# Twelve instead of eight K tiles of an mLSTM input projection in seven products, with a tanh output gate and rescheduled DRAM sums

## The chip, the cores and the metric

The kernel runs on one core of a Trainium2 chip. The metric is device time in microseconds (us) of one execution of the whole program. Before the change it is 2150.58 us, the median of three runs (2148.87 to 2151.29). TensorE multiplies matrices into PSUM; VectorE (DVE), ScalarE (ACT) and GpSimd (POOL) work on tiles in SBUF and read PSUM where they can; SyncE (SP) issues most weight loads. Each engine runs its own instructions in order.

## The reference

An encoder trunk of two layers on 256 positions of width 2048, in float32. Layer 0 mixes by pooling and attention, layer 1 by an mLSTM; each is followed by a gated MLP of width 5632 with a short convolution. The change is in the mLSTM mixer, cut here to what matters:

```python
proj = h @ w_in                                   # 2048 -> 4*2048 + 32
q = heads(proj[..., :2048]) * 256 ** -0.5         # 8 heads of 256
k = heads(proj[..., 2048:4096])
v = heads(proj[..., 4096:6144])
o_gate = jax.nn.sigmoid(proj[..., 6144:8192])
...                                               # scans forward and backward
hsum = (h_fw + h_bw).transpose(0, 2, 1, 3)
hn = hsum * lax.rsqrt(jnp.mean(hsum * hsum, axis=-1, keepdims=True) + NORM_EPS)
hn = hn * h_norm.reshape(8, 256)
y = (hn.reshape(b, s, 2048) * o_gate)
return y @ w_out
```

## The kernel before, in words

**Numbers in two parts.** Each weight tile of 128 partitions and 1024 columns (512 KB) is loaded into a raw buffer (seven of them, `wraw`). `Stream.split` then cuts it into a high part (a cast by ScalarE, L137) and a low part (a subtraction by VectorE, L138) in one of four `hl` buffers. A product is three matmuls: high by high, high by low, low by high. `Stream` loads six tiles ahead of the one in use and splits two ahead.

**The order of TensorE** is written out by hand. `Weave` keeps a clock that the groups of matmuls advance by their nominal time, and runs queued generators (heads, gates, drains) when they are due. A number that a generator yields is the time until it goes on. The order of the other engines is worked out by the scheduler of the framework from the program and the dependencies.

**The mLSTM layer** (`mlstm_layer`, L780) works on four pairs of heads, `hp` 0 to 3. For each it runs, head by head, the projections of q (`mq`) and k (`mk`), 16 K tiles each, and then the output gate of this pair together with the values of the next (`gates_values`, L986); the last pair has only its gate (`mo`). A `head` generator (L868) per head makes the masked weights (`arg`), the scores (`qk`), the normalised matrix `A`, its transposes (`atr`) and the result (`av`, `hn`). `gated` (L929) applies the output gate. It makes the sigmoid from an Exp on ScalarE (L932), an addition of one (L936) and two reciprocals per head (L938) on VectorE, multiplies (L942) and transposes (`htr`).

**Seven products.** In `gates_values`, two K tiles, two halves of the positions and two column blocks (512 of the gate, 512 of the values) would take eight products. For the first eight K tiles (four pairs of K tiles, `ML_PAIRS`), a scheme of Strassen's kind takes seven. The list `ML_ORDER` (L48) gives their order. A stands for four products of one pair of K tiles on two weight tiles, B for two products on one tile, P for two products of two pairs on one tile. D and E are direct: four products each on one tile, for the K tiles that are not in the scheme. The scheme needs sums of blocks of x (`combine`, L956, kept in `mcomb`) and of weights. `first` and `second` put the partial results together on VectorE.

**Sums of weights.** An A needs the tiles s0 + s1 and s0 + s1 + r. They are made in DRAM ahead of time by `premix` (L478): copies issued by ScalarE's queue, accumulating DMAs issued by GpSimd's queue, each paced by a matmul. Where both tiles are made there (`Made`, `Made`) this takes ten DMAs per pair of K tiles. Where only the first is (`Made`, `Chain`), it takes four, and the second comes from two additions on VectorE in SBUF (L133 and L134). Before, even pairs are of the first kind and odd ones of the second. Calls of `premix` set the start and the gap between the pairs:

```python
premix(0, 26.0, 33.0, 8)              # sums of feed-forward layer 0, from the attention on
premix(2, 30.0, 30.0, 0)              # mLSTM sums, after up group 27 of 44 of that layer
hp == 0 and premix(1, 30.0, 30.0, 0)  # sums of feed-forward layer 1
```

**The feed-forward layers** interleave `up` groups (64 matmuls) with products of the same seven-product scheme (`pp`) and drains into PSUM and SBUF. The other products are `op` (output projections) and `dn` (direct down projections).

Of the kernel before, what the change touches and what calls it, by code (L numbers as in the profile page):

```python
# [9 lines left out]
F32 = mybir.dt.float32  # L10
F32R = mybir.dt.float32r
AF = mybir.ActivationFunctionType
# [4 lines left out]
P = 128  # L17
# [29 lines left out]
ML_PAIRS = 4  # L47
ML_ORDER = [(e[0], int(e[1:] or 0)) for e in "A0 D A1 D A2 D A3 D B0 B1 B2 E B3 E P0 E P2 E".split()]  # L48
# [171 lines left out]
def trunk(ctx: ExitStack, tc: tile.TileContext, gx, xT, xn, call, catt, cml, weights, mixes, out):  # L220
# [56 lines left out]
    def rsqrt(ss, n, scale, name):  # L277
# [502 lines left out]
    def mlstm_layer(norm, nxt):  # L780
        with ExitStack() as es:
# [6 lines left out]
            comb = actp.tile([P, ML_PAIRS, 2, 4, P], F32R, tag="B1", name="mcomb")  # L788
# [79 lines left out]
            def head(h, q, kk, vt, hh):  # L868
# [34 lines left out]
                yield 10.0 if h % 2 else 6.0  # L903
# [20 lines left out]
                r = rsqrt(ss, 2, 1.0 / MD, f"h{h}")  # L924
# [4 lines left out]
            def gated(ps, heads, og=None):  # L929
                og = og or t1p.tile([P, 2, len(heads) * MD], F32, tag="og", name=f"og{heads[0]}")  # L930
                for t in range(2):
                    a.activation(og[:, t, :], ps[:, t, :], AF.Exp, scale=nrcol[:, t : t + 1])  # L932
                yield 1.2
                for i, h in enumerate(heads):
                    o = og[:, :, i * MD : i * MD + MD]
                    v.tensor_scalar_add(o, o, 1.0)  # L936
                    for t in range(2):
                        tc.keep_in_program_order(v.reciprocal(o[:, t], o[:, t]))  # L938
# [3 lines left out]
                    tc.keep_in_program_order(v.tensor_mul(hn, hn, o))  # L942
# [13 lines left out]
            def combine(j):  # L956
# [9 lines left out]
                a.copy(comb[:, j, 0], sf)  # L966
                v.tensor_sub(comb[:, j, 1], sf, comb[:, j, 0].bitcast(F32))
# [18 lines left out]
            def gates_values(hp):  # L986
# [44 lines left out]
                for kind, j in ML_ORDER:  # L1031
                    if kind == "A":
                        xs = [[comb[:, j][:, i, m] for i in range(2)] for m in (1, 0, 2)] + [x_part(2 * j + 1, 1)]
                    elif kind == "B":
                        xs = [x_part(2 * j + k, 0) for k in range(2)]
                    elif kind == "P":
                        xs = [[comb[:, j + k][:, i, 3] for i in range(2)] for k in range(2)]
# [23 lines left out]
            for hp in range(MH // 2):  # L1061
# [12 lines left out]
                if hp == 0:  # L1074
                    nrcol = kp.tile([P, 2], F32, tag="nrcol", name="nrcol")
                    v.tensor_scalar_mul(nrcol, norm.rcol, -1.0)
# [9 lines left out]
                hp == 0 and premix(1, 30.0, 30.0, 0)  # L1086
# [7 lines left out]
    def ffn_layer(layer, norm, nxt):  # L1094
        with ExitStack() as es:
# [194 lines left out]
            for kind, c, i, *j in _ffn_plan(layer):  # L1290
                if kind == "up":
# [4 lines left out]
                    if layer == 0 and (c, i) == (len(FCH) - 3, 6):  # L1296
                        premix(2, 30.0, 30.0, 0)
# [72 lines left out]
def _ml_weights(chunks, parts):  # L1370
# [6 lines left out]
    for hp in range(MH // 2):  # L1377
# [4 lines left out]
        for kind, j in ML_ORDER:  # L1382
# [6 lines left out]
            out += made + [Chain(part[2])] * (j % 2)  # L1389
# [226 lines left out]
```

## Time and profile before

| | |
|---|---|
| median of three runs | 2150.58 us |
| profiled execution | 2149.47 us, of which the span of instructions 2147.7 us |
| TensorE busy | 2141.0 us, 100% of the span |
| VectorE busy | 1809.6 us, 84% |
| ScalarE busy | 1443.1 us, 67% |
| GpSimd busy | 289.4 us, 13% |
| DMA | 606.66 MB, mean 282 GB/s |
| mLSTM projections of q to k and the gates, pairs 0 to 2 | about 1000 to 1274 us |

The stages of interest, by the start of their matmuls: feed-forward layer 0 from 261 us, the mLSTM from 968 us, its three windows of gates and values from 1041, 1134 and 1228 us, its output projection from 1345 us, feed-forward layer 1 from 1444 us. A row of the chain of waits gives a start, a length and the work that the end of the program hung on at that time. A row of groups gives the line, the engine, the operation with its operands and count, then the busy time, the mean length in ns, and the idle time of the engine before it. Matmuls overlap, so TensorE's busy time alone doesn't show its rate; the distance between starts does.

### The profile page before, as it was taken

How to read it: one execution, taken by the hardware profiler on the slowest of the kernel's cores; microseconds unless marked ns; L12 is line 12 of the kernel's file. 1: busy time of each engine (PE TensorE's matmuls, PEld its weight loads, DVE VectorE, ACT ScalarE, POOL GpSimd, SP SyncE). 2: the span in 40 equal slices, each digit the busy share in tenths (PEclk: the TensorE clock that was granted, in tenths of full speed). 3: DMA queues.
4: the chain of work that ended last, by engine and by line, in shares of the span. 5: the costliest groups of instructions: out<-in, count | busy, mean ns of one | idle time of the engine just before them, and what ended most of it. 6: DMA issues, size and time to landing. Idle time of an engine off the chain costs nothing.

```text
span 2147.7 us, 32376 instructions
## 1 busy us (share of the span) xinstructions
PE 2141.0 (100%) x11364; PEld 1834.4 (85%) x11364; DVE 1809.6 (84%) x2548; ACT 1443.1 (67%) x2199; POOL 289.4 (13%) x366
## 2 busy tenths in 40 slices
PE   9999999999999999999999999999999999999999
PEld 8888888888888888889888888888888888888887
DVE  7786678889998889898888897667888898889988
ACT  6665577777777767766556564557777777777774
POOL 0022112111111121111100011211111111100000
DMA  9678889899999999888878798988999999988775
GB/s 333 209 213 257 260 250 320 272 326 328 320 330 328 331 341 320 296 292 213 287 232 282 234 308 238 280 244 245 311 293 331 333 314 319 287 256 270 253 251 188
DMA packets 181542, 606.66 MB, mean 282 GB/s; under 512 B 23706, under 2 KB 26562, under 8 KB 181378
## 3 DMA queue, kind: packets, MB, share of 16 engines
q1 hardware_dynamic: 133952, 478.60, 61.6%
q0 software_dynamic: 28384, 70.54, 19.2%
q10 hardware_dynamic: 19042, 55.45, 7.8%
q8 instruction: 89, 1.46, 0.3%
q14 instruction: 75, 0.61, 0.1%
HBM read 602.35 MB, written 104.90 MB: 329 GB/s over the span
## 4 chain that ended last, share of the span: by engine, by line
PE 95%; DVE 3%; DMA 1%; issue 1%; ACT 1%; ACTq 0%; DVEq 0%
PE up L275 44%; PE pp L275 15%; PE op L275 8%; PE mq L275 4%; PE mk L275 4%; PE mo L275 3%; PE qproj L275 3%; PE mv L275 3%; PE dn L275 3%; PE mp L275 1%; DVE hl L138 1%; PE kproj L275 1%; PE vproj L275 1%; PE pool L275 1%; PE qk L275 1%
## 5 line engine op out<-in xcount | busy, mean ns | idle before, releaser
L138 DVE TENSOR_TENSOR hl<-w,hl 128x1024 fp32r<-128x1024 f32 (+1 forms) x869 | 1046.1, 1215 | 161.2 <-ACT hl L137 154.1
L137 ACT CAST hl<-w 128x1024 fp32r<-128x1024 f32 (+1 forms) x868 | 891.7, 1046 | 395.4 <-PE up L275 112.6
L275 PE MATMUL up<-xx,hl 128*128 128x512 f32 (+1 forms) x5632 | 993.8, 337 | 0.0
L275 PEld LDWEIGHTS up<-xx,hl 128*128 128x128 f32 x5632 | 866.9, 188 | 130.4 <-DVE hl L138 0.5
L491 POOL DMA_DIRECT2D m<-m x184 | 148.6, 826 | 924.2 <-PE up L275 442.6
L275 PE MATMUL pp<-hl,s 128*128 128x512 f32 x912 | 227.8, 391 | 1.6 <-DVE hl L138 1.2
L275 PEld LDWEIGHTS pp<-hl,s 128*128 128x128 f32 x912 | 167.7, 188 | 37.3 <-DVE hl L138 4.9
L275 PE MATMUL pp<-hl,g 128*128 128x512 f32 x684 | 174.0, 390 | 0.0
L275 PEld LDWEIGHTS pp<-hl,g 128*128 128x128 f32 x684 | 125.8, 188 | 24.5
L441 ACT COPY tb_up<-up 128x512 f32<-128x512 f32 x88 | 51.6, 587 | 116.0 <-PE up L275 116.0
L1126 DVE TENSOR_TENSOR y<-y,z 128x510 f32<-128x510 f32 x88 | 60.7, 690 | 63.0 <-ACT y L1125 62.5
L491 POOL DMA_DIRECT2D m<-in_dn x80 | 70.0, 875 | 267.8 <-PE up L275 57.0
L1125 ACT ACTIVATE y<-tb_up,conv 128x256 f32<-128x256 f32 x176 | 103.8, 590 | 0.0
L275 PE MATMUL mk<-xx,hl 128*128 128x512 f32 (+1 forms) x512 | 92.5, 338 | 0.0
L442 DVE TENSOR_TENSOR tb_up<-up,tb_up 128x512 f32<-128x512 f32 x88 | 60.8, 690 | 37.4 <-ACT tb_up L441 37.1
L275 PE MATMUL mq<-xx,hl 128*128 128x512 f32 (+1 forms) x512 | 92.0, 337 | 0.0
L1123 ACT ACTIVATE z<-tb_up,conv 128x256 f32<-128x256 f32 x176 | 88.4, 502 | 5.3 <-DVE tb_up L1118 3.4
L275 PE MATMUL op<-hl,cat 128*128 128x512 f32 x384 | 91.5, 393 | 0.0
L275 PE MATMUL op<-hl,mcat 128*128 128x512 f32 x384 | 89.7, 392 | 0.0
L275 PEld LDWEIGHTS mq<-xx,hl 128*128 128x128 f32 x512 | 79.2, 188 | 11.6
L275 PEld LDWEIGHTS mk<-xx,hl 128*128 128x128 f32 x512 | 79.1, 188 | 11.4
L1124 ACT ACTIVATE z<-tb_up,conv 128x256 f32<-128x256 f32 x176 | 87.5, 497 | 0.0
(258 smaller groups left out, 2209.3 us busy)
## 6 DMA issues: line engine op xcount, KB each, us to landing
w<-in_up SPq DMA_DIRECT2D x352, 512.0 KB, 6.6
w<-in_dn SPq DMA_DIRECT2D x174, 512.0 KB, 6.0
w<-in_m_in SPq DMA_DIRECT2D x118, 512.0 KB, 5.3
w<-m SPq DMA_DIRECT2D x98, 512.0 KB, 5.7
m<-in_dn ACTq DMA_DIRECT2D x160, 256.0 KB, 5.7
m<-m POOLq DMA_DIRECT2D x184, 128.0 KB, 6.0
w<-in_a_in SPq DMA_DIRECT2D x45, 512.0 KB, 5.6
m<-in_dn POOLq DMA_DIRECT2D x80, 256.0 KB, 7.1
```

What stands on the lines that cost most here:

```text
L137: (self.nc.vector.tensor_copy if i + c == 0 else self.nc.scalar.copy)(hl[:, 0, c : c + n], w[:, c : c + n])
L138: low = self.nc.vector.tensor_sub(hl[:, 1, c : c + n], w[:, c : c + n], hl[:, 0, c : c + n].bitcast(F32))
L275: last_mm[0] = pe.matmul(out_, lhsT, rhs, start=start, stop=stop, skip_group_check=True)
L441: a.copy(tb, ps[:, :, 1, :])
L442: v.tensor_add(tb, ps[:, :, 0, :], tb)
L491: paced(eng.dma_start(to[p : p + P // 2], src[p : p + P // 2], **kw))
L1123: a.activation(z[:, 0, j, :], u[:, j, :], AF.Copy, scale=cw(tl, 0))
L1124: a.activation(z[:, 1, j, :], u[:, j, :], AF.Copy, scale=cw(tl, 2))
L1125: a.activation(y[:, j, :], u[:, j, :], AF.Identity, scale=cw(tl, 1), bias=cw(tl, 3))
L1126: v.tensor_add(y[:, :, 1:S], y[:, :, 1:S], z[:, 0, :, 0 : S - 1])
```

## The change

- `ML_PAIRS` goes from 4 to 6: K tiles 0 to 11 of the gate and the values of pairs 0 to 2 are in seven products, and only tiles 12 to 15 are direct. `ML_ORDER` is written anew. The sums of x for the two added pairs get a second buffer, `mcomb1`; the split q of a head gets one buffer in place of two.
- The sums for pair `hp` 2 are all of the kind `Made`, `Chain`.
- The sigmoid is written as half of one plus the tanh of half the argument. ScalarE takes Tanh; the addition of one is part of the multiplication on VectorE; the factor one half is put into the constants of `rsqrt`. The addition and the reciprocals go.
- The two generators' gaps between the matrix `A` and its transposes go from 6 and 10 to 9 and 14.
- The mLSTM sums start after up group 36 of feed-forward layer 0 instead of 27, and follow each other by 18 instead of 30. The sums of feed-forward layer 1 start after the gates of pair 1 instead of pair 0, by 28 instead of 30.

```diff
-ML_PAIRS = 4
-ML_ORDER = [(e[0], int(e[1:] or 0)) for e in "A0 D A1 D A2 D A3 D B0 B1 B2 E B3 E P0 E P2 E".split()]
+ML_PAIRS = 6
+ML_ORDER = [(e[0], int(e[1:] or 0)) for e in "A0 A1 D A2 A3 A4 D A5 B0 B1 B2 B3 B4 E B5 P0 P2 E P4".split()]
...
-        v.tensor_scalar(t, ss, scale, EPS, ALU.mult, ALU.add)
+        v.tensor_scalar(t, ss, scale / by**2, EPS / by**2, ALU.mult, ALU.add)
...
-            comb = actp.tile([P, ML_PAIRS, 2, 4, P], F32R, tag="B1", name="mcomb")
+            combs = [actp.tile([P, 4, 2, 4, P], F32R, tag="B1", name="mcomb0")]
+            combs.append(kp.tile([P, ML_PAIRS - 4, 2, 4, P], F32R, tag="mcomb", name="mcomb1"))
...
-                r = tp.tile([P, 2, 2, S], F32R, tag=name[0] + "hl", name=f"hl_{name}")
+                r = tp.tile([P, 2, 2, S], F32R, tag=name[0] + "hl", bufs=2 - (name[0] == "q"), name=f"hl_{name}")
...
-                yield 10.0 if h % 2 else 6.0
+                yield 14.0 if h % 2 else 9.0
...
-                r = rsqrt(ss, 2, 1.0 / MD, f"h{h}")
+                r = rsqrt(ss, 2, 1.0 / MD, f"h{h}", 0.5)
...
-                    a.activation(og[:, t, :], ps[:, t, :], AF.Exp, scale=nrcol[:, t : t + 1])
+                    a.activation(og[:, t, :], ps[:, t, :], AF.Tanh, scale=hrcol[:, t : t + 1])
...
-                    v.tensor_scalar_add(o, o, 1.0)
-                    for t in range(2):
-                        tc.keep_in_program_order(v.reciprocal(o[:, t], o[:, t]))
-                        yield 2.5
...
-                    tc.keep_in_program_order(v.tensor_mul(hn, hn, o))
+                    tc.keep_in_program_order(v.scalar_tensor_tensor(hn, o, 1.0, hn, ALU.add, ALU.mult))
...
-                hp == 0 and premix(1, 30.0, 30.0, 0)
+                hp == 1 and premix(1, 28.0, 28.0, 0)
...
-                    if layer == 0 and (c, i) == (len(FCH) - 3, 6):
-                        premix(2, 30.0, 30.0, 0)
+                    if layer == 0 and (c, i) == (len(FCH) - 2, 7):
+                        premix(2, 18.0, 18.0, 0)
...
-            made = [Made()] if j % 2 else [Made(), Made()]
+            made = [Made()] if j % 2 or hp == 2 else [Made(), Made()]
```

More of the change, by code (lines that the diff above doesn't have):

```diff
@@ L1032, in gates_values @@
                     if kind == "A":
-                        xs = [[comb[:, j][:, i, m] for i in range(2)] for m in (1, 0, 2)] + [x_part(2 * j + 1, 1)]
+                        xs = [[comb(j)[:, i, m] for i in range(2)] for m in (1, 0, 2)] + [x_part(2 * j + 1, 1)]
                     elif kind == "B":
@@ L1036, in gates_values @@
                     elif kind == "P":
-                        xs = [[comb[:, j + k][:, i, 3] for i in range(2)] for k in range(2)]
+                        xs = [[comb(j + k)[:, i, 3] for i in range(2)] for k in range(2)]
                     else:
@@ L1385, in _ml_weights @@
                 continue
-            made = [Made()] if j % 2 else [Made(), Made()]
+            made = [Made()] if j % 2 or hp == 2 else [Made(), Made()]
             part = [p[hp * ML_PAIRS + j] for p in parts]
             mixes.append(part + [made])
-            out += made + [Chain(part[2])] * (j % 2)
+            out += made + [Chain(part[2])] * (2 - len(made))
     return out, mixes
```

12 lines of the change are left out of this document (7 added, 5 removed).

## The prediction

> **What bounds the kernel now.** First the chain of waits. In it eighteen matmuls of 128x512 take 4.09 us, 0.227 us each, with no gap between pieces: TensorE's own issue rate is the time.
>
> ```profile
> 341.03 4.09 PE pp L275 x18
> ...
> 713.71 11.15 PE up L275 x64
> 734.90 3.84 DMA w<-in_up
> 745.28 10.05 DMA w<-in_dn
> 764.90 11.25 PE up L275 x64
> 776.15 4.09 PE pp L275 x18
> 780.24 11.14 PE up L275 x64
> ```
>
> The chain leaves TensorE in one place of weight, in the first feed-forward layer. Between 713.71 and 764.90 stand three groups of 64 (11.14 each) and 66 matmuls of products (18, 24 and 24): 33.4 + 15.0 = 48.4 us of work in 51.2 us. So 2.8 us are lost there, behind weights that landed 10 us after their issue.
>
> Then the stages, one row for each: length, busy time of TensorE, its weight loads, VectorE (DVE), ScalarE (ACT) and GpSimd (POOL), granted clock, DMA share, GB/s.
>
> ```profile
> 560.00:680.00 120.00, 120.00 (x643) 103.10 (x643) 108.02 (x143) 86.15 (x129) 19.17 (x24) 1.00 1.00 327
> 680.00:765.00 85.00, 83.70 (x439) 70.05 (x437) 72.63 (x96) 60.12 (x93) 16.88 (x21) 1.00 1.03 331
> 809.00:850.00 41.00, 41.00 (x219) 35.17 (x218) 38.27 (x52) 31.07 (x49) 8.06 (x10) 1.00 1.03 339
> 850.00:925.00 75.00, 75.00 (x400) 64.38 (x400) 65.50 (x83) 53.07 (x78) 7.02 (x9) 1.00 0.91 291
> 1000.00:1040.70 40.70, 40.70 (x242) 35.73 (x241) 32.65 (x63) 21.88 (x26) 3.87 (x5) 1.00 0.92 268
> 1040.70:1086.70 46.00, 46.00 (x224) 38.78 (x223) 41.60 (x69) 30.21 (x43) 6.25 (x8) 1.00 0.88 279
> 1133.60:1179.75 46.15, 46.15 (x221) 38.74 (x220) 41.23 (x67) 29.54 (x39) 3.54 (x5) 1.00 0.91 303
> 1227.70:1273.78 46.08, 45.40 (x215) 37.76 (x214) 41.00 (x66) 29.37 (x38) 6.52 (x8) 1.00 0.92 303
> 1273.78:1321.20 47.42, 47.42 (x286) 41.92 (x285) 39.22 (x61) 25.67 (x35) 7.90 (x10) 1.00 0.86 255
> ```
>
> Rows six to eight are the three gates-and-values windows that the change rewrites. TensorE is busy throughout except 0.68 us in the third. VectorE stands at 41.0 to 41.6 us, some 90%: it has 4.4, 4.9 and 5.1 us to spare per window, and that margin is what the change spends. The 0.68 us idle begins with a weight tile issued at 1225.21; what it costs stays in my sum, since the same queues meet there again.
>
> ```profile
> 1225.21 4.34 DMA w<-in_m_in
> ...
> 1231.31 3.70 PE mo L275 x15
> ```
>
> **Matmuls.** Per pair of heads the products go from 7x4 + 8x4 = 60 to 7x6 + 4x4 = 58. Three pairs save six products of three matmuls each, eighteen of 128x512: exactly the first row above, -4.09 us, all on the path.
>
> **Weight tiles and VectorE.** A window's tiles go from 8 (A) + 4 + 4 + 4 (B, D, E) + 2 (P) = 22 to 12 + 6 + 2 + 2 + 3 = 25. Each extra one costs a cast on ScalarE and a subtraction on VectorE. The tiles summed in SBUF ("Chain", two additions each) go from 2 per window to 3, 3 and 6.
>
> ```profile
> L138 DVE TENSOR_TENSOR hl<-w,hl 128x1024 fp32r<-128x1024 f32 x857 | 1036.5, 1221 | 160.9 <-ACT hl L137 153.8 <-DMA w<-in_m_out 3.0 <-DMA m<-in_dn 1.5
> ...
> L137 ACT CAST hl<-w 128x1024 fp32r<-128x1024 f32 x857 | 883.8, 1050 | 393.6 <-PE up L275 112.6 <-PE op L275 61.0 <-issue 29.8
> ...
> L133 DVE TENSOR_TENSOR w<-w,w 128x512 f32<-128x512 f32 x6 | 4.1, 683 | 0.0
> ```
>
> VectorE gets 3 x 1.22 = 3.7 us per window, and 2 x 0.68 = 1.37 us per further Chain: 1.4, 1.4 and 5.5 us. ScalarE gets 3 x 1.05 us on 30 of 46, beside other work.
>
> **The gate by tanh.** An addition and two reciprocals per head go; the multiply with the output gate becomes one with an addition inside, on the same operands, taken at the price of the third row.
>
> ```profile
> L938 DVE RECIPROCAL og<-og x16: 1692/1742/1746, 1085.1 to 1363.7; 128x256 f32<-128x256 f32 x16
> L936 DVE TENSOR_SCALAR og<-og x8: 418/419/427, 1083.3 to 1348.0; 128x512 f32<-128x512 f32 x8
> L942 DVE TENSOR_TENSOR hn<-hn,og x8: 675/682/685, 1094.5 to 1366.4; 128x512 f32<-128x512 f32 x8
> ```
>
> That is 0.42 + 2 x 1.74 = 3.9 us per head, 31 us of VectorE, but nearly all at the end of a window or after it, under the next heads' projections. Inside a window fall two of the additions and about one reciprocal: 2.6 us. The activation keeps its count and shape. If Tanh needed tables of its own, each group of gates between two Exp would load them twice, at most 8 loads; the nearest row is the load that Exp needed after Ln, 1283 ns.
>
> ```profile
> L833 ACT ACT_TABLE_LOAD x1 | 1.3, 1283 | 4.2 <-DMA gd<-gr 4.2
> ```
>
> I take no load. At both ends the path pays nothing: one load is shorter than the least cover of a weight tile, 2.1 us, shown next. The Trainium skill ("ScalarE: Activation LUTs", section on table sets) lists tanh beside exp in one set, so by it no load is added; no run here shows Tanh, and the reload after Ln shows that a function which the page places in a set with exp can still cost one.
>
> **The sum for VectorE.** First window: 41.6 + 3.7 + 1.4 - 2.4 (one addition and the larger part of a reciprocal less, by its end) = 44.2 of 46.0 - 1.36 = 44.6 us. Second: 41.2 + 3.7 + 1.4 - 2.6 = 43.7 of 44.8. Third: 41.0 + 3.7 + 5.5 - 2.6 = 47.6 of 44.7. The first two fit, just; the third is 2.8 us over. What is ready ahead helps little once tiles are used up every 1.36 us (six matmuls) instead of in turn with a D tile that lasts twelve:
>
> ```profile
> 1137.52 2.52 DVE L138 TENSOR_TENSOR hl<-w,hl 128x1024 fp32r<-128x1024 f32 x2
> ...
> 1140.81 2.20 PE L275 MATMUL mp<-hl,mcomb 128*128 128x512 f32 x9
> ```
>
> The second of these subtractions ends at 1140.04 for the tile used from the seventh matmul, 1142.17: 2.1 us of cover, after a single D. The new order has A0 A1 and A2 A3 A4 in a row. Bounds for windows one and two: 0 if packed, 4.0 and 3.8 us if today's idle VectorE time is unavoidable (44.2 + 4.4 - 44.6; 43.7 + 4.9 - 44.8). For the third: 0 if the five last additions of a set (3.4 us) slide into the next stage, where VectorE is at 39.2 of 47.4; 7.9 us at the other end. I take 0, 0 and 2.8, the packed values, since the windows with most to do leave least idle.
>
> **The DRAM sums, first the mLSTM's.** They now begin nine `up` groups later, 18 us apart instead of 30, and there are 18 of them for 12. Six prepare two tiles (six DMAs of 256 KB and four of 128: 2.1 MB), and twelve instead of six prepare one (four of 256: 1.05 MB).
>
> ```profile
> m<-in_dn ACTq DMA_DIRECT2D x160, 256.0 KB, 5.7
> m<-m POOLq DMA_DIRECT2D x184, 128.0 KB, 6.0
> ```
> ```profile
> 677.85 0.50 ACTq L491 DMA_DIRECT2D m<-in_m_s  x1
> ```
>
> The first one now is issued at 677.85: it falls into the sums of the first feed-forward layer (2.1 MB per 33 us, 64 GB/s) and adds 1.57 MB per 30 us, 52 GB/s. The stretch 560 to 680 moved 327 GB/s, so 680 to 765 asked for 379 and got 331. Over 85 us that is 4.1 MB late, 7.8 tiles of 0.52 MB, of which the six loaded ahead cover six; 1.8 tiles at 331 GB/s are 2.8 us, the loss found above. After the change the first sum falls near 809 (the 36th `up` is the last row of the chain above and ends at 791.4), behind the other sums, so those 2.8 us go (bounds 0 and -2.8; I take -2.8). The new stretch asks for 339 - 52 + 87 = 374 for 41 us and 326 after: 35 x 41 = 1.4 MB, 2.7 tiles, covered. Without the cover it costs 1.4 MB / 339 = 4.2 us. The last sum then starts near 1115 and is done near 1160, ahead of its load near 1215.
>
> **The sums of the second feed-forward layer** start one pair of heads later, every 28 us instead of 30: 75 GB/s, not 70, and the last is ready near 1880, its A products being due after 1960. In the third window loads and sums ask for 25 x 0.52 / 44.7 + 75 = 368 GB/s against 339 as seen: 1.3 MB, 2.5 tiles, covered; uncovered 3.8 us. Taken 0.
>
> **Queues.** Twelve more issues on ScalarE's queue (0.50 us in the row at 677.85), twelve on GpSimd's, nine on SyncE's. GpSimd is at 3.5 to 6.5 us of a window; behind its paced DMAs wait the heads' small power operations, and longer head gaps (9 and 14 for 6 and 10) cover those. SyncE's loads wait in order: a late sum holds the loads behind it, hence the dates above. Two more combinations of x (under 7 us of VectorE at 0.68 per operation) fall into 1000 to 1040, with 8 us idle. One buffer less for q makes its cast wait for the scores of the head before, at most their 1.6 us, with tiles 7 us ahead. The factor one half sits in constants. All 0 on the path. Later PE positions of the transposes remove no matmul.
>
> **Sum.** -4.1 - 2.8 + 2.8 = -4.1 us on the profiled execution (span 2147.7, device 2149.47): 2145.4. The median of the runs is 1.1 us above that execution, so 2146.5, a ratio of 0.9981. About 0.2% (4.3 us) is what a measurement of this kernel tells from no change; my sum ends just short of it.
>
> **Rivals.** (1) VectorE catches up: the last additions slide out and no window waits, -6.9: 2143.7. For it: the slack of the stage behind; against it: A2 A3 A4 in a row. (2) The late loads reappear after 809 or in the windows, so that the 2.8 us are only moved: 2149.3. For it: 374 GB/s asked; against it: the cover of six tiles. (3) Slower: VectorE becomes the bound of all three windows with its idle waits kept, 4.0 + 3.8 + 7.9 = 15.7 us: -6.9 + 15.7 = +8.8, 2159.4. It ends above 0.2% once the windows lose 11.2 us together, 3.7 each. For it: 2.1 us of cover; against it: the 560 to 680 row, VectorE at 108 of 120 with TensorE never idle. (4) Memory traffic: a sum reads and writes, so the 560 to 680 row carried 327 + 64 = 391 GB/s without idle, and the third window asks 293 + 75 + 75 = 443. The 52 over make 2.3 MB, under the 3.1 MB loaded ahead: no loss if 391 holds, 5.9 us if the cover fails, 2152.4. The Trainium skill ("DMA: Bandwidth & Descriptors", Specifications) puts a core's share of HBM at about 358 GB/s; the 391 disagrees, and by the page the third window would lack 3.8 MB, 1.9 us beyond the cover, 2148.4.
>
> **Chances.** My sum 0.54, its spread split evenly by the bound at 2146.3; rival 1 0.18; rival 2 with the gentle form of 4 0.15; rival 3 with the full loss of 4 0.13. Faster 0.27 + 0.18 = 0.45, same 0.27 + 0.15 = 0.42, slower 0.13. The sum's own range is 2144 to 2149. The range of 8 in 10 runs from 2142, a little below rival 1, to 2154, past rivals 2 and 4, and leaves out the far half of rival 3.
>
> **What would show it.** 522 matmuls instead of 540 in the products of the three windows; no DMA piece in the chain near 745; the first sum near 809; VectorE at 98% of the first two windows and TensorE waiting for a subtraction (L138) in the third, at A3 or A4; no reciprocal of 1.74 us. Wrong it would be if TensorE waits in all three windows for VectorE, if weights land later than 8 us there, if new table loads stand between the heads, or if the chain shows DMA after 809.

## The result, and the profile after

The changed kernel takes 2157.90 us (median of six runs, 2155.86 to 2158.98) against 2150.11 us before (six runs): a ratio of 1.0032, 95% interval 1.0022 to 1.0043. It is slower by 7.8 us where 4.1 us of gain were forecast, and outside the range. The profiled execution took 2158.14 us, with a span of 2156.3.

Two expected gains are there. The first is read from the chain of waits of the changed kernel (start, length, work) in the first feed-forward layer.

```profile
713.73 11.13 PE up L275 x64
...
728.95 11.14 PE up L275 x64
740.09 5.45 PE pp L275 x24
745.54 11.14 PE up L275 x64
756.67 5.45 PE pp L275 x24
762.12 11.14 PE up L275 x64
```

From 713.73 to 762.12 are 48.39 us, the 48.4 of work that the prediction counted there; the pieces of DMA at 734.90 and 745.28 are gone. The second is the count of matmuls, in the page's first part, the kernel before on the first line, the changed one on the second:

```profile
PE 2141.0 (100%) x11364; PEld 1834.4 (85%) x11364; DVE 1809.6 (84%) x2548; ACT 1443.1 (67%) x2199; POOL 289.4 (13%) x366
```
```profile
PE 2140.4 (99%) x11346; PEld 1832.6 (85%) x11346; DVE 1800.9 (84%) x2555; ACT 1453.6 (67%) x2210; POOL 298.3 (14%) x378
```

Eighteen matmuls fewer, and VectorE has 8.7 us less to do. The stages of the mLSTM, from the view that gives busy times by stretch (length, busy TensorE, weight loads, VectorE, ScalarE, GpSimd, granted clock, DMA share, GB/s), show where the time went; the last three rows are the windows of gates and values:

```profile
1000.00:1040.00 40.00, 37.80 (x220) 32.53 (x219) 29.34 (x59) 19.80 (x24) 6.20 (x8) 1.00 0.98 267
1042.00:1091.00 49.00, 44.47 (x205) 36.49 (x205) 41.94 (x70) 32.59 (x45) 10.28 (x12) 0.97 0.93 301
1139.00:1184.00 45.00, 42.50 (x205) 34.73 (x204) 37.52 (x63) 28.63 (x42) 4.65 (x6) 1.00 0.96 301
1233.00:1278.00 45.00, 44.13 (x217) 36.80 (x216) 41.89 (x70) 30.47 (x42) 3.20 (x3) 1.00 0.89 300
```

TensorE stands idle 2.2, 4.5, 2.5 and 0.9 us, the least of it in the third window, where the prediction had put all of it. VectorE is not at 98% of the first two windows but at 86% and 83% (73% in the first row, 93% in the last), so it was not short of time there: it waited for something too.

To compare stages I use one more quantity, worked out from the trace: the distance between the starts of neighbouring matmuls, less what one of that shape takes at full rate (0.227 us for 512 columns), added up. It counts idle TensorE and a halved clock alike. Each row is one profiled execution. That of e17_chains12 is its slowest run (2151.32 us, 3.0 above its median), that of e3_sums_alone lies 2.2 above and that of e18_pause 2.3 below; the others are within 0.7 us of their medians. In us:

| kernel | 700-800 | 800-1000 | 1000-1050 | 1050-1100 | 1150-1200 | 1200-1300 | whole program |
|---|---|---|---|---|---|---|---|
| before | 4.31 | 3.10 | 1.32 | 0.42 | 0.47 | 2.33 | 38.3 |
| after | 1.48 | 3.12 | 10.33 | 2.18 | 4.17 | 2.96 | 50.8 |
| e1_combos | 1.47 | 3.07 | 5.55 | 3.40 | 2.06 | 3.07 | 45.1 |
| e17_chains12 | 1.48 | 3.08 | 3.47 | 1.39 | 4.95 | 3.11 | 44.0 |
| e18_pause | 1.47 | 4.63 | 1.55 | 4.97 | 1.73 | 3.02 | 43.9 |
| e21_pause_chains | 1.48 | 3.86 | 1.30 | 8.46 | 1.95 | 2.96 | 47.4 |
| e24_no_sums | 1.48 | 3.06 | 1.34 | 1.44 | 1.57 | 2.98 | 38.4 |
| e25_chains_nosums | 1.47 | 3.07 | 2.21 | 1.44 | 1.58 | 2.99 | 39.6 |
| e3_sums_alone | 1.48 | 4.55 | 7.53 | 0.31 | 0.38 | 2.35 | 43.0 |
| e20_sums_pause | 1.48 | 3.20 | 3.49 | 0.82 | 0.48 | 2.35 | 38.1 |

After against before: 12.5 us more lost and 18 x 0.227 = 4.1 us less work make +8.4, and the spans differ by 8.6. The first feed-forward layer gives 2.8 back, so the rest loses 15.3 us in this execution: 10.8 in the first pair of heads (1000 to 1100), 3.7 in the second window and 0.6 in the third; the 0.2 left over lies elsewhere.

### The profile page after: what moved, and what is told of

Its sections match the earlier page's. It is cut to its first block, busy times and chain, and to the rows that moved or that the text cites. A ratio compares the mean times of both kernels' runs of the same rounds, so it can differ in the third digit from the quotient of the medians.

```text
span 2156.3 us, 32440 instructions
## 1 busy us (share of the span) xinstructions
PE 2140.4 (99%) x11346; PEld 1832.6 (85%) x11346; DVE 1800.9 (84%) x2555; ACT 1453.6 (67%) x2210; POOL 298.3 (14%) x378
## 4 chain that ended last, share of the span: by engine, by line
PE 92%; DVE 4%; DMA 2%; issue 1%; ACT 1%; ACTq 0%; DVEq 0%
PE up L275 44%; PE pp L275 16%; PE op L275 8%; PE mq L275 4%; PE mk L275 4%; PE qproj L275 3%; PE dn L275 3%; PE mv L275 2%; DVE hl L138 2%; PE mo L275 1%; PE kproj L275 1%; PE vproj L275 1%; PE pool L275 1%; PE xt L326 0%; DMA w<-in_m_in 0%
## 5 line engine op out<-in xcount | busy, mean ns | idle before, releaser
L138 DVE TENSOR_TENSOR hl<-w,hl 128x1024 fp32r<-128x1024 f32 (+1 forms) x878 | 1057.0, 1216 | 174.2 <-ACT hl L137 168.7
L137 ACT CAST hl<-w 128x1024 fp32r<-128x1024 f32 (+1 forms) x877 | 899.9, 1046 | 386.2 <-PE up L275 116.4
L442 DVE TENSOR_TENSOR tb_up<-up,tb_up 128x512 f32<-128x512 f32 x88 | 60.8, 691 | 38.4 <-ACT tb_up L441 37.9
```

Of the source, the lines that this page charges most:

```text
L137: (self.nc.vector.tensor_copy if i + c == 0 else self.nc.scalar.copy)(hl[:, 0, c : c + n], w[:, c : c + n])
L138: low = self.nc.vector.tensor_sub(hl[:, 1, c : c + n], w[:, c : c + n], hl[:, 0, c : c + n].bitcast(F32))
L442: v.tensor_add(tb, ps[:, :, 0, :], tb)
```

## The experiments

Three theories stand. **Order:** work of the first pair stands in the wrong place in TensorE's or VectorE's order. **Traffic:** the denser DRAM sums make other transfers late. **VectorE** (the prediction's): it has too much to do. All results in one table; the ratio is to the kernel before on the same chip, whose median went from 2149.1 to 2151.1 over the chips used. Where a gain of one kernel over another is given, it is the difference between their distances to that median. The ratio is a separate estimate from the same runs. It differs from the quotient of the medians by up to 0.0009, some 2 us (e20_sums_pause stands 0.7 us below the kernel before by the medians and at 1.0000 by the ratio), so parts of 1 to 3 us are rough.

| run | edit, in short | median us | ratio | 95% interval |
|---|---|---|---|---|
| e1_combos | after; combinations done when the sixth is issued | 2151.86 | 1.0008 | 0.9999 to 1.0017 |
| e2_behind | after; SBUF additions two subtractions later | 2157.53 | 1.0042 | 1.0027 to 1.0057 |
| e3_sums_alone | before; mLSTM sums late and close | 2151.98 | 1.0014 | 1.0004 to 1.0024 |
| e4_sums_early | after; sums at the old start | 2174.80 | 1.0123 | 1.0108 to 1.0138 |
| e8_both | e1 + e2 | 2154.44 | 1.0016 | 1.0007 to 1.0024 |
| e10_gload | e1; G on GpSimd's queue | 2152.03 | 1.0008 | 1.0000 to 1.0017 |
| e11_exp | e1; gate by Exp | 2152.82 | 1.0007 | 0.9998 to 1.0016 |
| e13_sums_gload | e3; G on GpSimd's queue | 2151.31 | 1.0000 | 0.9991 to 1.0009 |
| e17_chains12 | e1; additions later in windows 1 and 2 | 2148.32 | 0.9993 | 0.9984 to 1.0002 |
| e20_sums_pause | e3; sums held near the gates | 2148.86 | 1.0000 | 0.9991 to 1.0008 |
| e16_best | four edits | 2153.72 | 1.0023 | 1.0012 to 1.0033 |
| e19_best2 | four edits, with the hold | 2152.72 | 1.0012 | 1.0004 to 1.0021 |
| e18_pause | e1; sums held | 2153.48 | 1.0018 | 1.0009 to 1.0027 |
| e21_pause_chains | e17; sums held | 2154.44 | 1.0025 | 1.0015 to 1.0035 |
| e22_first | e21; p4, p6 freed sooner | 2153.12 | 1.0020 | 1.0010 to 1.0029 |
| e23_gaps | e21; old head gaps | 2154.85 | 1.0031 | 1.0019 to 1.0042 |
| e24_no_sums | e21; last seven sums left out | 2146.20 | 0.9984 | 0.9975 to 0.9993 |
| e25_chains_nosums | e17; last seven sums left out | 2146.84 | 0.9989 | 0.9980 to 0.9998 |

**The combinations of x.** `gates_values` begins with `wv.until("combos" in done)`. The flag is set 8 us of the hand-kept clock after the last combination. With six instead of four that moment lies behind the place where the first window begins, so the clock is put forward to it, and head 0's generator, which is due by that clock, places its groups ahead of the matmuls that were to cover them.

```diff
                     combine(j)
-                    yield 8.0
+                    if j < ML_PAIRS - 1:
+                        yield 8.0
```

> The changed kernel, but the sums of x count as finished when the sixth is issued, not 8 us of the hand-kept clock later. Theory 1 (the wait for them sets that clock 2.8 us ahead at the first window, so the transposes and the A-times-v matmuls of head 0 stand too early in TensorE's order): the waits of 1.0, 2.6 and 1.4 us at 1041 to 1048 go, the time falls by about 5 us, from 7.9 us above the kernel before to about 3. Theory 2 (VectorE is simply full in the first window): the waits move to weight tiles and the time stays within 1.5 us of the changed kernel.

2151.86 us, and the waits of this `av` group behind ScalarE and VectorE are gone. TensorE's order, from the timeline view (start, length, engine, operation, the idle time before it and its releaser), first in the changed kernel:

```profile
1041.32 0.66 PE L912 MATMUL atr<-cst,A 128*128 128x128 f32 x4 [0.87 <-DVE A L904]
1041.73 1.64 PE L275 MATMUL mp<-hl,mcomb 128*128 128x512 f32 x6
1045.80 0.50 PE L275 MATMUL av<-mvt,at 128*128 128x256 f32 x2 [2.43 <-ACT at L914]
1047.56 2.50 PE L275 MATMUL av<-mvt,at 128*128 128x256 f32 x10 [1.25 <-DVE at L915]
```

and in e1_combos:

```profile
1040.18 0.66 PE L912 MATMUL atr<-cst,A 128*128 128x128 f32 x4 [0.68 <-DVE A L904]
1040.59 1.62 PE L275 MATMUL mp<-hl,mcomb 128*128 128x512 f32 x6
1043.96 0.97 PE L275 MATMUL mo<-hl,xx 128*128 128x512 f32 x3 [1.75 <-DVE tb_k L442]
1044.76 1.53 PE L275 MATMUL mp<-hl,mcomb 128*128 128x512 f32 x6
1046.13 1.75 PE L275 MATMUL av<-mvt,at 128*128 128x256 f32 x12
```

With the edit nine more matmuls stand between the transposes and `av`, and `av` waits for nothing. One wait of 1.75 us, for VectorE's `tb_k`, stands in their place. This is the largest single part of the loss, 6.2 us by the medians (7.8 - 1.6), and it is order, not work. In the two profiled executions 4.8 of it lie between 1000 and 1050 and 2.1 in the second window, while 1.2 more are lost from 1050 to 1100; why the second window gains is not shown.

**The additions in SBUF.** In VectorE's order an addition (L133) stands behind the subtraction of four tiles before, and waits there for its own raw tile. The edit puts it two subtractions later (some expectations call it one tile later).

```diff
-            self.behind(self.nc.vector.tensor_add(w[:, :half], ...), self.lows[0])
+            self.behind(self.nc.vector.tensor_add(w[:, :half], ...), self.lows[2])
```

> The changed kernel, but the two additions of a weight tile summed in SBUF are ordered behind the subtraction two tiles before instead of four. Theory 1 (in VectorE's order the additions stand before their weights have landed and hold up what is behind them): VectorE's waits of 3.2 and 3.0 us for these weights at 1035 and 1159 shrink below 1 us each and the second window's 2.2 us of TensorE idle go; the time falls by 2 to 4 us. Theory 2 (VectorE is full, the order is of no account): no change beyond 1 us, or slower, since the additions now fall closer to their use.

> e1_combos with the additions of the summed tiles one tile later in VectorE's order (as in e2_behind). Theory: VectorE no longer waits for raw tiles near 1033, 1059 and 1153 (3.3, 2.5, 1.2 us), so the windows of the first two pairs lose about 2 us less, but the third, where all six sums are made so, loses about 4 more than in e1_combos, as in e2_behind: 2152.5 to 2155. Rival: in the third window e2_behind lost because heads stood too early, not because VectorE was short; then e8_both stands at 2149 to 2151.

The row of L133 among the groups (busy us and mean ns, then the idle time of VectorE before it and what ended it), after and e2_behind:

```profile
L133 DVE TENSOR_TENSOR w<-w,w 128x512 f32<-128x512 f32 x12 | 8.2, 686 | 6.2 <-DMA w<-in_m_s 6.2
```
```profile
L133 DVE TENSOR_TENSOR w<-w,w 128x512 f32<-128x512 f32 x12 | 8.2, 687 | 0.0
```

VectorE's wait of 6.2 us goes, and yet the kernel is no faster (2157.53): the third window, where all six second tiles are made so, now waits. TensorE's waits between 1228 and 1275 in e2_behind (us in total, times, longest); the changed kernel has no wait for L138 or L137 there:

```profile
PE mp L275 <- DVE hl L138: 3.0, 5, 0.9
PE mp L275 <- ACT hl L137: 0.6, 2, 0.3
```

e8_both has these waits to the same tenth with head 0 in its right place, so the rival of its expectation (that the heads made the third window late) falls. The edit in the first two windows alone keeps the one and not the other:

```diff
-    def __init__(self, src):
-        self.src = src
+    def __init__(self, src, at=0):
+        self.src, self.at = src, at
...
-            self.behind(self.nc.vector.tensor_add(w[:, :half], ...), self.lows[0])
+            self.behind(self.nc.vector.tensor_add(w[:, :half], ...), self.lows[self.srcs[i].at])
...
-            out += made + [Chain(part[2])] * (2 - len(made))
+            out += made + [Chain(part[2], 2 * (hp < 2))] * (2 - len(made))
```

> e1_combos with the additions of summed tiles one tile later in VectorE's order in the first two windows alone. Theory (there they make VectorE wait for raw tiles, and the third window is short of VectorE only if they stand late there too): the TensorE waits at 1061.63 and 1063.43 (1.6 us together) and VectorE's idle 3.3 and 2.5 us go, the third window loses 2 us as in e1_combos and not 5.4: 2149 to 2151. Rival (VectorE is short in all windows, so that what goes in one place comes back in the next): 2151.5 to 2154.

2148.32 us against 2149.60 for the kernel before beside it: -1.3 us, where e1_combos stands at +1.6 and the change at +7.8. It is the fastest version of the whole computation, well ahead of the change and not told apart from the kernel before. The intervals of e1_combos and e17_chains12 just overlap (0.9999 to 1.0017 and 0.9984 to 1.0002), so the 2.9 us between them are likely, not certain. The waits named in the expectation went. New is one of 2.4 us in the second window, told of below.

**The sums.** The late start and the small gap alone, in the kernel before, and the old start in the change:

```diff
-                    if layer == 0 and (c, i) == (len(FCH) - 3, 6):
-                        premix(2, 30.0, 30.0, 0)
+                    if layer == 0 and (c, i) == (len(FCH) - 2, 7):
+                        premix(2, 18.0, 18.0, 0)
```

> The kernel before with only the mLSTM's DRAM sums moved: begun after the 36th group instead of the 27th, 18 us apart instead of 30. If the loss of 2.8 us in the first feed-forward layer comes from two sets of sums at once, it goes: 2.8 us faster than the kernel before, TensorE's rate in 700 to 800 as elsewhere. If denser sums late cost as much as they save: no difference, with new waits in the mLSTM between 1000 and 1050.

> The changed kernel with its DRAM sums 18 us apart but begun after the 27th group, as before. They are then done before the mLSTM's first window. If the late landings in the mLSTM (7 to 10 us at 996, 1065 and 1151) come from the sums beside them, the waits at 1014 and 1160 (2.3 and 2.2 us) go, while the first feed-forward layer loses its 2.8 us again, or more as the sums are denser: between 2 us faster and 3 us slower than the changed kernel. If the waits come from the order of the engines, they stay and the time rises by 3 us or more.

e3_sums_alone gains the 2.8 us in the first feed-forward layer and loses 6.2 from 1000 to 1050: a wait of 3.1 us for `cols`, and from its end on (1005.55 to 1012.38) 6.83 us at half clock. Its chain there:

```profile
996.86 6.84 DMA gd<-gr
...
1004.11 0.45 ACT L833
...
1005.41 0.43 ACT rows_b L833
...
1005.88 1.07 PE cols L275 x4
```

The store `gd` of 40 KB takes 6.8 us. In the kernel before, the load that waits for it was issued 2.3 us after it (999.0 and 1001.3). ScalarE issues that load and stands still until then. The chain of the changed kernel has the same store, then the load of G behind it (twice some 7 us), and ends in a wait of 2.2 us for `mk` at 1014:

```profile
996.13 7.14 DMA gd<-gr
...
1003.72 7.16 DMA G<-gd
...
1012.91 1.14 DVE hl L138
...
1014.10 2.60 PE mk L275 x14
```

e4_sums_early loses 17 us more than the change (if the sums were at fault, 3 at most were expected), nearly all between 700 and 800: its chain has a weight tile of 14.98 us there.

```profile
716.88 14.98 DMA w<-in_dn
```

In its mLSTM the wait of 1.7 us in the second window is gone, but its gates, with pieces of sums landing until 1026, still wait 4.2 us for `cols`. So beginning later is worth 2.8 us and more where the sums are dense. The question was whether the place of the small load or the sums' traffic is at fault. Its load from another queue, in the change (with e1's edit) and in the kernel before:

```diff
-                    a.dma_start(G[:, d, :], gd[r : r + 1, :].to_broadcast([P, S]))
+                    (a if h else g).dma_start(G[:, d, :], gd[r : r + 1, :].to_broadcast([P, S]))
```

> The changed kernel with two edits: the sixth combination of x counts as done when it is issued (as in e1_combos), and head 0 loads its gate rows G from GpSimd's queue, not ScalarE's. Theory (ScalarE stands blocked behind the late 40 KB store gd<-gr): its idle 3.8 us near 1003 go, the TensorE waits at 1012.47 (1.10 us) and 1043.96 (1.91 us) of e1_combos shrink by at least half, time 2149.5 to 2150.7, that is 1.2 to 2.4 below e1_combos. Rival (the sums' memory traffic itself makes the tiles late, whichever engine issues the small load): waits stay, 2151.5 to 2152.3.

> The kernel before with the mLSTM sums begun as late and as close as in the change (as in e3_sums_alone), and head 0's G loaded from GpSimd's queue. Theory: the 6.2 us that e3_sums_alone lost between 1000 and 1050, half-clock stretch included, go back to the 1.3 of the kernel before, the 2.8 us gained in the first feed-forward layer stay, less about 1.4 near 952: 2148 to 2149.5. Rival (traffic): the wait of the cols matmul near 1005 and the half clock stay, 2151.5 to 2152.5.

ScalarE is free, but the store is as late as before and VectorE waits in its place (e10_gload, groups between 1000 and 1100):

```profile
L883 DVE SCALAR_TENSOR_TENSOR arg<-G,mc,kml 128x128 f32<-128x128 f32 x6 | 2.1, 346 | 3.1 <-DMA G<-gd 3.1
L879 POOL DMA_DIRECT2D G<-gd x2 | 1.1, 574 | 7.0 <-DMA gd<-gr 7.0
```

e10_gload is no faster than e1_combos. e13_sums_gload stands 1.5 us below e3_sums_alone, with intervals that overlap; 1.0 of it lies before 1000, and the wait of 3.1 us for `cols` has become one of 3.3 for `mk`. The theory of a blocked ScalarE falls. Instead, the copies and accumulations of the sums are held back while these transfers pass:

```diff
                 for p in range(0, P, P // 2):
+                    while hold:
+                        yield 1.0
                     paced(eng.dma_start(...))
...
             def gates(ps):
+                hold.append(1)
...
                 yield 6.0 if h == 0 else 2.5
+                hold.clear()
```

> The kernel before with the late, close sums of the change (as in e3_sums_alone), and no copy of a sum issued from the start of the gates' work until head 0 has its gate rows. Theory (the sums in flight make the 40 KB store and the gate rows behind it late): gd lands within 4 us of its issue, not 6.9; the wait of the cols matmul (3.28 us) and the stretch at half clock go, 1000 to 1050 loses 1 to 2.5 us, not 7.5; time 2147 to 2149.5. Rival (the place of G on ScalarE's or GpSimd's queue, or VectorE, sets it): the wait only changes its place and 2151 to 2152.5 stands.

2148.86 us, 0.7 below the kernel before where e3_sums_alone was 1.7 above; the load of G is issued 3.3 us after the store, and the chain from 990 to 1016 is TensorE alone (e20_sums_pause):

```profile
990.41 10.45 PE mq L275 x60
1000.86 1.01 PE cols L275 x8
```

So the sums in flight make the store late. By the ratio e13_sums_gload and e20_sums_pause are not told apart (1.0000 each); it is the trace that separates them: from 1000 to 1050 e13 loses 6.4 us, near the 7.5 of e3_sums_alone, and e20 3.5. Not all of the 2.8 us comes back as time: 2.2 us are lost at 1037, where head 0's transposes wait for A.

**Putting the cures together.** This failed four times.

> Four edits on the change: combinations counted done when the sixth is issued; head 0's G from GpSimd's queue and 14 us, not 6, before VectorE uses it; the additions of the first two windows one tile later; the first E tile after B5, not B4. By the theories the waits of e1_combos at 1012 (1.10), 1044 (1.91), 1061 and 1063 (1.60) and those for the mvf tile (0.96, 0.72, 0.71) go, 7.0 us together, on 2151.9: 2144 to 2147. Rival (VectorE short): what is taken away comes back as waits for subtractions, 2149 to 2152.

> As e16_best, but with G on ScalarE's queue and 6 us as in the change, and instead no copy of a sum issued from the start of the gates' work until head 0 has its gate rows. If the sums in flight are what makes gd late, as good as e16_best or better: 2143.5 to 2147. If not, ScalarE stands blocked for some 4 us near 1003 as in e1_combos, and 1.1 to 3 us of e16_best's gain are missing: 2147 to 2149.5.

> e1_combos with no copy of a sum issued from the start of the gates' work until head 0 has its gate rows. If the sums in flight made gd late here as in e20_sums_pause: gd lands in 4 us, the waits at 1012 (1.1 us) and 1044 (1.9 us) go, 2148.5 to 2150. Rival (the sums held back come later, at the cost of the first window's weights): ScalarE waits for weights near 1064 to 1080 as in e19_best2, TensorE at 1066 to 1090, and 2151.5 to 2154.

> e18_pause with the additions of the first two windows one tile later in VectorE's order, that is e19_best2 with the first E tile where the change has it, ahead of B5. If E behind B5 was the fault of e19_best2 (its waits of 2.47 us at 1079 and 1.0 us near 1164): 2146 to 2148.5. Rival (the hold is the fault, since late weights of the first window follow it): 2150.5 to 2153.

The first two have the moved E tile, `"... B4 B5 E P0 P2 E P4"`; e18 and e21 have not, and are no faster, so E was not the fault. In e18, e19 and e21 the hold does what it should: 1.3 to 1.6 us lost from 1000 to 1050, as before the change. But 5.0 to 8.7 are lost in the next 50. The chain of e21_pause_chains:

```profile
1062.35 13.67 DMA w<-in_m_in
...
1076.12 1.05 ACT hl L137
...
1077.20 1.23 DVE hl L138
1078.43 0.61 DVE mvf L1026
...
1079.17 4.54 PE mv L275 x12
```

A weight tile of the first window lands 13.7 us after its issue. ScalarE's cast, VectorE's subtraction and, behind it in VectorE's order, the operation that frees the tile of p4 and p6 follow, and the `mv` group waits 4.5 us. The load is issued on SyncE's queue, where no copy of a sum stands. The copies held back were issued from 1024 on and met the window. e16_best has no hold and loses 5.0 and 7.4 us in the same two stretches; which of its edits does that isn't settled.

Is it traffic, or the order of the queues? The last seven of the eighteen sums are left out, with all loads and products in place:

```diff
         for i, e in enumerate(mixes[layer]):
+            if layer == 2 and i >= 11:
+                for to, src in zip(e[-1], (e[0], e[2])):
+                    to.ap = src
+                continue
```

> e21_pause_chains without the last seven of the eighteen sums in DRAM (their tiles are loaded straight from the first term, so the last A tile of the second window and the A tiles of the third hold other numbers and the output is not the reference's); loads, products, casts and subtractions stay as they are. Theory (traffic of the sums makes the first window's weights late): weights land in 6 to 8 us between 1040 and 1100, not 10 to 12, the waits near 1070 to 1081 (5.6 us) go but for 1 to 2 us, and the time falls by 5 to 8 us: 2147 to 2149.5. Rival (order of the queues or VectorE): within 1.5 us of e21_pause_chains, 2153 to 2156.

> e17_chains12 without the last seven of the eighteen sums in DRAM (their tiles come straight from the first term, so the output is not the reference's). Theory: the wait of 2.54 us at 1169 with its stretch at half clock, behind ScalarE's wait of 3.15 us for a weight tile, goes; the wait at 1013 (2.06 us) stays, since two sums are still in flight there; 2144.5 to 2147, which is what the products are worth if the added sums cost nothing. Rival: within 1 us of e17_chains12, 2147.5 to 2149.5.

e24_no_sums falls to 2146.20, 3.2 us below the kernel before where e21 is 5.3 above, and its chain in that place has no DMA:

```profile
1068.50 0.59 DVE mvf L1030
...
1072.11 3.00 PE mv L275 x12
```

The loads of the first window (1040 to 1100, KB each, median us from issue to landing) in the kernel before, e21_pause_chains and e24_no_sums:

```profile
w<-in_m_in SPq DMA_DIRECT2D x25, 512.0 KB, 4.9
```
```profile
w<-in_m_in SPq DMA_DIRECT2D x24, 512.0 KB, 9.8
```
```profile
w<-in_m_in SPq DMA_DIRECT2D x27, 512.0 KB, 7.9
```

The median fell by less than was expected, to 7.9, at the far end of the 6 to 8; the late tiles are what went. The DMA engines are full in this stretch in e21 and nearly so without the sums:

```profile
1040.00:1100.00 60.00, 54.85 (x260) 44.85 (x259) 49.94 (x79) 37.95 (x52) 14.95 (x18) 0.97 1.01 319
```
```profile
1040.00:1100.00 60.00, 59.55 (x306) 50.13 (x305) 55.22 (x85) 41.99 (x57) 11.61 (x13) 1.00 0.97 309
```

e25_chains_nosums ends at 2146.84, -2.6 us where e17 has -1.3. In its profiled execution the wait at 1169 is gone. The chain of e17_chains12 there shows what it was:

```profile
1156.34 9.60 DMA w<-in_m_in
...
1169.15 4.29 PE mv L275 x12
```

The wait at 1013, which was expected to stay, went from 2.1 to 0.8 us, by the distance between starts. The two executions differ by 4.6 us, the medians by 1.3, with intervals that overlap almost wholly: the profile of e17_chains12 is of its slowest run, and how often the wait at 1169 occurs is not shown.

**The other parts of the change.** The gate, by Exp as before, on e1_combos:

```diff
-                r = rsqrt(ss, 2, 1.0 / MD, f"h{h}", 0.5)
+                r = rsqrt(ss, 2, 1.0 / MD, f"h{h}")
...
-                    a.activation(og[:, t, :], ps[:, t, :], AF.Tanh, scale=hrcol[:, t : t + 1])
+                    a.activation(og[:, t, :], ps[:, t, :], AF.Exp, scale=hrcol[:, t : t + 1])
...
+                    v.tensor_scalar_add(o, o, 1.0)
+                    for t in range(2):
+                        tc.keep_in_program_order(v.reciprocal(o[:, t], o[:, t]))
+                        yield 2.5
...
-                    tc.keep_in_program_order(v.scalar_tensor_tensor(hn, o, 1.0, hn, ALU.add, ALU.mult))
+                    tc.keep_in_program_order(v.tensor_mul(hn, hn, o))
...
-                    v.tensor_scalar_mul(hrcol, norm.rcol, 0.5)
+                    v.tensor_scalar_mul(hrcol, norm.rcol, -1.0)
```

> e1_combos with the output gate as before the change (Exp, one addition and two reciprocals per head). If VectorE is what the windows wait for, the 2.6 us of additions and reciprocals inside each window lengthen all three, by 1 to 2.6 us each: 2154.5 to 2158. Rival: the gate's work lies under the next heads' projections, as the prediction said of most of it, and the time stays within 1 us of e1_combos, 2151 to 2153.

A ratio of 1.0007 against e1's 1.0008: 31 us less on VectorE are worth nothing that can be measured. The profiled execution of e11 (2155.90, 3.1 above its median) lost 3.5 us more than that of e1, but the medians don't show it. Two last edits on e21_pause_chains, the operations that free p4 and p6 closer together and the old head gaps:

```diff
                     a.copy(t5, tiles["p5"])
-                    yield 1.2
+                    yield 0.5
...
                         tc.keep_in_program_order(op(to, one, two))
-                        yield 1.0
+                        yield 0.4
```
```diff
-                yield 14.0 if h % 2 else 9.0
+                yield 10.0 if h % 2 else 6.0
```

> e21_pause_chains with the three operations that free the tile of p4 and p6 issued closer behind A5 (0.5 and 0.4 us apart in the plan, not 1.2 and 1.0). Theory: the three waits of the mv group (0.7 to 0.95 us each) shrink by half or more, 1 to 2 us below e21_pause_chains. Rival (VectorE's queue of subtractions sets them, not the plan): within 0.5 us of e21_pause_chains.

> e21_pause_chains with the head gaps of the kernel before (10 and 6 for 14 and 9). If the longer gaps are needed in the new windows (the transposes would wait for A, the av group for its copies): 1 to 4 us above e21_pause_chains. Rival: VectorE is done with A in 6 us in either, so within 0.7 us.

e22 ends 1.3 us below e21, with overlapping intervals. Its `mv` wait in the first window stays (4.8 us), since a late tile sets it; the two in the later windows go, while `av` waits more. e23 is not told apart from e21 either. Its profile shows the trade: in the third window the transposes wait for A, which none does in e21,

```profile
PE atr L918 <- DVE A L910: 2.1, 1, 2.1
```

and the second window loses 0.6 us, not 2.0.

## Why the prediction was wrong

**Matmuls, -4.09: right.** 18 fewer, and in e24_no_sums, where nothing else is lost on balance (38.4 us against 38.3), the span is 3.9 us shorter than before.

**The first feed-forward layer, -2.8: right**, in place, size and cause. The first sum is issued at 807.8, forecast near 809. Every kernel with the late start has the 2.8 us (4.31 to 1.48 in the table).

**VectorE, 0, 0 and +2.8: wrong in its place.** In the third window VectorE was nearly full (41.9 of 45.0 us) and yet no tile was late for long; it lost 0.6 us. In its middle:

```profile
1236.00:1264.00 28.00, 28.00 (x137) 23.45 (x137) 26.95 (x50) 19.46 (x26) 0.71 (x1) 1.00 0.83 291
```

That its margin was thin was right: e2_behind and e8_both spent it by moving the additions two subtractions. How many of the additions slid into the next stage was not measured. The first two windows and the heads ahead of the first lost 14.5 us with VectorE at 73 to 86%. Packing was the wrong question for them: VectorE was held up in its order, by an addition that waits for its raw tile (6.2 us idle), and its cure in the first two windows is worth 2.9 us by the medians (e1 against e17).

**"Two more combinations of x ... All 0 on the path": the step that failed most**, 6.2 us. The work of VectorE was priced, 7 us of it in a stretch with 8 idle, and that was not the cost. The combinations are also a date of the hand-kept clock, and the prediction never asked what waits for `done`.

**"The DRAM sums ... covered", taken 0: the second step that failed.** Rates were compared over a stretch (374 against 339 GB/s) with six tiles loaded ahead set against the shortfall. From 809 to 850 that held: 325 GB/s were moved there and nothing more was lost (3.12 against 3.10 us from 800 to 1000). But a store of 40 KB has no tiles loaded ahead, and neither has the load behind it. Cost, by the medians: 2.4 us at the gates (e3 against e20), 1.3 for the last seven sums (e17 against e25, not told apart), and 8.5 once the held sums meet the first window (e21 against e24). The first of these is also the failure of **"Queues"**: ScalarE's queue was counted by its issues of 0.50 us, not by the load that waits in it for a store. The sums also ended later than forecast: the last piece landed at 1202, not near 1160, still ahead of its load.

**A term that was missing:** the `mv` group waits for the tile of p4 and p6, 0.96, 0.72 and 0.71 us in e1_combos. Five B tiles between A5 and E, 5 x 6 x 0.227 = 6.8 us, do not cover it. These three waits remain in e24_no_sums. With one of `av` they are most of the 2.8 us that its profiled execution loses in the windows beyond the kernel before. By its median it misses the full gain of 6.9 (rival 1) by 3.7: e24's -3.2 us stands near the prediction's -4.1 by luck, since the prediction's loss was to come from VectorE in the third window.

**Tanh without a table load, 0: right.** ScalarE loads tables three times between 985 and 1400, at the gates as before, and none stands between the heads; the activation kept its 0.72 us.

**The rivals.** Rival 3 gave a time near the one measured (2159.4), by a mechanism that did not happen: VectorE did not bound three windows. Rivals 2 and 4 had the kind of cause that the sums turned out to be, late loads through memory traffic, at 2.8 and 5.9 us. Rival 2 put it after 809 or in the windows, rival 4 in the third window; from 800 to 1000 and in the third window no more than 0.6 us was lost, and neither named the gates.

By the medians the change loses 7.8 + 4.1 + 2.8 = 14.7 us. Of these the runs account for 6.2 (combinations), 2.9 (additions) and, not told apart from nothing, 1.3 (the last seven sums); the `mv` waits are 2.4, read from a profile. The 1.9 us that are left fit the late store. Its cost in time was measured on the kernel before only (2.4). In the changed kernel the hold took 4.0 us (e1 to e18) and 2.2 us (e17 to e21) out of 1000 to 1050, by the table of distances, but brought a larger loss 60 us later. So the order of head 0 and the harm done by the sums are shown; the split of the last 4 us is not.

## What to carry to other kernels

Where the order of an engine is planned by a clock of one's own, every added piece of work is also a date: look for what waits until it is done, and compare the planned order itself before and after, not the busy times. Background traffic is priced by what else is in flight when the smallest dependent transfer passes, not by the mean rate of a stage; and traffic held back is paid where it comes out. If an engine is 85% busy and its consumers wait, read what that engine waited for before counting its work.

## What the runs showed of the hardware

**The clock can halve after waits of 1.75 us and more.** After the waits of 2.4 and 1.3 us at 1045, TensorE of the changed kernel ran at half its clock for 3.42 us; after the wait of 4.5 us, e21_pause_chains the same. The rows by stretch, with the granted clock third from the end:

```profile
1047.37:1050.79 3.42, 3.23 (x13) 3.04 (x14) 3.07 (x5) 0.69 (x4) 0.00 (x0) 0.50 0.85 287
```
```profile
1079.08:1082.49 3.41, 3.32 (x8) 2.67 (x9) 0.25 (x1) 1.33 (x4) 0.00 (x0) 0.50 1.01 393
```

The twelve `mv` matmuls that take 3.00 us in e24 take 4.54 in e21, so this wait cost about 1.5 us more than itself. The shortest single wait with a half clock behind it was 1.75 us (e11_exp, at 1063, then 3.41 us at a granted clock of 0.50), the next 2.0 us (e18_pause, at 1060). One of 1.75 us in e1_combos, at 1044, and one of 2.2 us in the changed kernel, at 1014, had none. In e3_sums_alone the half clock lasted 6.83 us. The Trainium skill ("TensorE: Matmul & The Clock Gate", Part 1) describes a free-running window of 3.4 us whose idleness sets the clock to one half; the stretches of 3.41 and 3.42 us agree with that length, and the one of 6.83 with twice it. Its rule in the section on HAM oscillation, that gaps above some 3.4 us are to be avoided, is too mild by these runs, where 1.75 us was enough at times; the measurement decides.

**A small transfer is slowed by others in flight.** The store of 40 KB took 6.8 us in e3_sums_alone and 7.1 in the changed kernel; in the kernel before and where the sums were held back the load behind it was issued after 2.3 to 3.3 us. In e3_sums_alone no copy of a sum was issued on ScalarE's queue between 985 and the store at 996.86, only on GpSimd's, so its place behind others in one queue is not the reason.
